# Splits ahead of the routing weights and norm roots by a GpSimd power in a two-layer mixture-of-experts encoder

## The chip, the cores and the metric

The kernel runs on one core of one Trainium2 chip. The metric is device time in microseconds (us) of a whole execution. TensorE (PE) multiplies matrices; VectorE (DVE), ScalarE (ACT) and GpSimd (POOL) work on tiles of 128 partitions; SyncE (SP) issues most of the transfers. Each engine takes its instructions in program order and waits where an input is missing.

## The reference, cut to what matters

512 tokens of width 1024 pass through two layers. In each, four attention mixers (`mla`, `dil`, `gqa`, `diff`) of four heads work on the normed input; their outputs are normed, joined, projected and added to the stream. A second norm feeds a router and 16 experts:

```
def rms_norm(x, gain):  x * rsqrt(mean(x * x) + 1e-6) * gain
...
g_prob = softmax(t @ wg + bg)                 # 4 groups: the best one is taken
e_logits = (t @ we + be)[best group]          # 4 experts in it: the best two
e_w, e_idx = top_k(softmax(e_logits), 2)
gate = one_hot(experts) * g_w * e_w / sum(e_w)
for e in range(16):
    hid = silu(t @ w_gate[e]) * (t @ w_up[e])
    y = y + gate[:, e:e + 1] * (hid @ w_down[e])
x = x + y
```

The weights are fp32: 1024 x 512 for gate and up, 512 x 1024 for down, per expert.

## The kernel before, in words

**Products.** Every fp32 product is three matmuls of a narrower type: each operand is split into a rounded `hi` and a rest `lo`, and `mm3` (L268) adds hi·hi, lo·hi and hi·lo. Weights arrive by SP's transfers in units of 128 x 1024 fp32 (`raw`). `W.split` turns the next units into `hi` (a copy on ACT, L144) and `lo` (a subtract, L145, on VectorE, or on POOL where it is called with G). It may run up to six units ahead of the unit in use (`HL`); a matrix of an expert is four units, and one unit is six matmuls.

**End of attention.** The order of the steps between the last attention units and the first expert is written by hand in `TAIL`: entries 57 to 69, run one after another by `tail`, each a list of words. A word is a letter, a token tile (0 to 3) and perhaps an engine (V or G): `o` and `d` open and close the out-projection of a tile, `r` is the root of the second norm, `e` the transposes for the router, `f` the router's logits, `h` the normed rows (`h30` a first part on POOL, `h31` the rest on ACT), `p` ranks the logits and counts each token's place in its expert's list, `x` picks the first expert's tokens by a matmul with a selection matrix, `l` makes the list of the second expert, `s` splits one unit, `T` splits the picked tokens into `xh` and `xl`, `K` computes the routing weights (`weights`, from L1333 to L1358), `m` clears a tile, `B` writes the last rows of the stream, `O` loads the number of overflow rounds into a register of each engine (L1470), `q` copies token numbers, `S` starts the gather of the second expert.

**Experts.** The matrices are worked through in the order g0 u0 g1 d0 u1 g2 d1 u2 and so on (`MOE_ORDER`; g is gate, u up, d down). Before each unit the loop splits ahead to the limit. At fixed units it makes the list of a later expert: `listed` forms the selection matrices (`hots`, four operations of L341), `start` multiplies them with the token numbers (`pli`, L1381), reads the list and gathers the rows. For every expert e this is done for e + 3 at u0 and u2. In expert 0 it is done beside that for expert 2 at g2 and u0, and for experts 0 and 1 (whose tokens have been picked already, but whose output rows and weights are still wanted) at u0 and u2.

**Roots.** `rstd` returns 1/sqrt(mean + eps) without ScalarE: a scale, an integer guess and three Newton rounds. The first three operations are on VectorE; the rounds are three operations each on VectorE (L133 to L135), or four each on POOL (L137 to L140) if E is G. It serves the first norm (`r0`, `r1`), the low-rank norm (`ra`), query and key heads (`rq`, 24 to 64 columns), the mixers' outputs (`yr`) and the second norm (`r2`). The third mixer's rope is on POOL (L430 to L445), behind VectorE's multiply by the root (L428). `kst` (L507) is a copy on POOL that TensorE transposes for the next head.

Of the kernel before, what the change touches and what calls it, by code (L numbers as in the profile page):

```python
# [44 lines left out]
        66: "e1 sG c2",  # L45
        67: "f0 b3G o2 p0 r1V f1 h1 d2 o3 r2G e2 x0 p1 c3 d3 f2 e3 h30 x1 r3G p2 h2 f3",
        68: "x2 h31 p3 l x3",
        69: "T K m sG B O q sG S"}
WAITP = 5
JOIN = 52  # L50
STORES = ((13, 0, 1), (6, 1, 2), (1, 2, 3), (0, 3, 4))
HOLD = 2
MIX = "gg" + "dg" * 8 + "gggggg"
CP = 704
# [8 lines left out]
def hybrid_encoder(ctx: ExitStack, tc: tile.TileContext, I: dict, out: bass.AP, depth=2, dbg=None):  # L63
# [18 lines left out]
    tokb = cst.tile([128, NT, 2], BF, name="tokb")  # L82
    wlast = cst.tile([128, NT], FT, name="wlast")
    brep = drm.tile([8, 128, 1024], FT, name="brep")

    def late_constants():
# [33 lines left out]

    def rstd(pool, ss, n, inv, name, E=V):

        x = "" if E is V else "g"
        v = pool.tile([128, n], FT, name=name + "v", tag="rsv" + x, bufs=1)
        y = pool.tile([128, n], FT, name=name + "y", tag=name + "y")
        f = pool.tile([128, n], FT, name=name + "f", tag="rsf" + x, bufs=1)
        ti = pool.tile([128, n], I32, name=name + "i", tag="rsi" + x, bufs=1)
        V.tensor_scalar(v, ss, inv, EPS, op0=OP.mult, op1=OP.add)
        V.tensor_scalar(ti, v.bitcast(I32), 1, None, op0=OP.logical_shift_right)
        V.tensor_scalar(y.bitcast(I32), ti, -1, 0x5f3759df, op0=OP.mult, op1=OP.add)  # L130
        for _ in range(3):
            if E is V:
                V.scalar_tensor_tensor(f, v, -0.5, y, op0=OP.mult, op1=OP.mult)  # L133
                V.tensor_tensor(f, f, y, op=OP.mult)
                V.scalar_tensor_tensor(y, f, 1.5, y, op0=OP.add, op1=OP.mult)  # L135
            else:
                E.tensor_tensor(f, y, y, op=OP.mult)  # L137
                E.tensor_tensor(f, f, v, op=OP.mult)
                E.tensor_scalar(f, f, -0.5, 1.5, op0=OP.mult, op1=OP.add)
                E.tensor_tensor(y, y, f, op=OP.mult)  # L140
        return y
# [181 lines left out]
    for layer in range(depth):  # L323
# [32 lines left out]
        with ExitStack() as c2:  # L356
# [425 lines left out]
            with ExitStack() as c3:  # L782
# [134 lines left out]
                def finish(mi):  # L917
# [3 lines left out]
                    if mi == 2:  # L921
# [3 lines left out]
                        yield LATER  # L925
                        r = rstd(sm, ss_, NT, 1.0 / 256, "yr", G)
                        for t in range(NT):
# [10 lines left out]
                    else:  # L938
                        for t in range(0, NT, 2):
# [3 lines left out]
                            V.tensor_reduce(ss_[:, t:t + 2], sq, axis=AX.X, op=OP.add)  # L943
                        r = rstd(sm, ss_, NT, 1.0 / 256, "yr", G)
                        yield LATER
# [12 lines left out]
                def finish_pair():  # L958

                    sl = slice(768, 896)  # L960
                    y = Y[3][:, :, :128]
                    yv = y.rearrange("p t (h d) -> p t h d", h=2)
                    sq = sm.tile([128, 512], FT, name="sq", bufs=1).rearrange("p (t h d) -> p t h d", t=NT, h=2)
                    ss_ = sm.tile([128, NT, 2], FT, name="yss")
                    G.tensor_tensor(sq, yv, yv, op=OP.mult)
                    yield LATER
                    V.tensor_reduce(ss_, sq, axis=AX.X, op=OP.add)
                    r = rstd(sm, ss_.rearrange("p t h -> p (t h)"), NT * 2, 1.0 / 64, "yr", G)
# [20 lines left out]
                def norm_pair(t, E):  # L989
                    sl, y = slice(896, 1024), Y[3][:, t, 128:]  # L990
                    r = rstd(sm, late['yss', t], 2, 1.0 / 64, "yr", E)
                    if E is V:
# [17 lines left out]
                def norm_x(t, E):  # L1010
                    V.tensor_scalar(ss2[:, t, 0:1], ss2[:, t, 0:1], ss2[:, t, 1:2], None, op0=OP.add)
                    late['r', t] = rstd(sm, ss2[:, t, 0:1], 1, 1.0 / D, "r2", E)

# [43 lines left out]
                def logits(t):  # L1057
                    pl = ps.tile([128, 512], FT, name="pl", tag="tr")[:, :20]
                    for k in range(8):
                        PE.matmul(pl, late['xT'][t % 2][:, k], late['wr'][:, k], start=k == 0, stop=k == 7)  # L1060
                    V.scalar_tensor_tensor(lg[:, t], pl, late['r', t], late['brg'][:, :20], op0=OP.mult, op1=OP.add)

# [25 lines left out]
                def route(t):  # L1088


                    l4 = lg[:, t].rearrange("p (r e) -> p r e", e=4)
# [5 lines left out]
                    for k, op in enumerate((OP.is_gt, OP.is_ge)):  # L1097
# [5 lines left out]
                    V.scalar_tensor_tensor(M[:, t].rearrange("p (g e) -> p g e", g=4), rank[:, t, 4:].rearrange("p (g e) -> p g e", g=4),  # L1103
                                           2.0, goh[:, t, :, None].to_broadcast([128, 4, 4]), op0=OP.is_lt, op1=OP.mult)
                    pp = ps.tile([128, 512], FT, name="pp", tag="tr")
                    for u in range(t + 1):
                        PE.matmul(pp[:, :NE], tri[:, 0 if u == t else 1], M[:, u], start=u == 0, stop=u == t)
# [5 lines left out]
                    V.tensor_scalar(late['oh'][:, t], iota, pos[:, t, 0:1], None, op0=OP.is_equal)  # L1113
                    if t == NT - 1:
                        oh1 = scr[:, 1536:1536 + NT * CAP // 2].bitcast(BF).rearrange("p (t c) -> p t c", t=NT)
                        late['oh1'] = hots(1, oh1)
                        count_rounds(pp[:, NE:2 * NE])

# [27 lines left out]

                STAGES = dict(l=list_rows, b=norm_pair, c=turn_pair, o=open_out, d=close_out, e=turn_x, r=norm_x, f=logits, h=normed,
                              p=route, x=pick, s=lambda E: W.split(W.done + 1, E), w=warm)
# [151 lines left out]
        with ExitStack() as c2:  # L1300
# [226 lines left out]
            for e, m in MOE_ORDER:  # L1527
                us = wbase[layer, e, m][0]
                for i, u in enumerate(us):
# [142 lines left out]
```

## Time and profile before

| | |
|---|---|
| median of three runs | 1393.4 us (1389.81 to 1403.58) |
| profiled execution | 1398.48 us |
| its span | 1396.6 us |
| mean granted TensorE clock | 0.966 of full speed |
| HBM read, written | 264.34 MB, 24.81 MB |

The rows below come from the profiled execution. Times are us from the start of its span; the span is the time between the first and the last instruction, and some 2 us of the execution lie around it. A timeline row gives start, busy time, engine, line of the kernel, operation, output and inputs, and in brackets the engine's idle time ahead of it with the instruction or queue that ended it. A name with q (ACTq) is an engine's sequencer: register loads and waits, not counted as busy. PEclk is the granted clock of TensorE, 1.00 for 2.4 GHz and 0.50 for 1.2 GHz.

### The profile page before, as it was taken

Reading aid. Unit: us, or ns where it says so; the run is one execution under the profiler, and the core shown is the slowest. Engines: PE = TensorE matmul, PEld = TensorE weight load, DVE = VectorE, ACT = ScalarE, POOL = GpSimd, SP = SyncE. Lnnn points to the kernel's source line nnn. Section 1 sums busy time; section 2 is a strip of 40 time slices with the busy share of each in tenths; the row PEclk is TensorE's granted clock in tenths of the full one; section 3 lists DMA queues with packets and bytes.
Section 4 is the critical chain, followed back from the end, with each engine's and each line's share of the span. In section 5 each row is a group of like instructions: output and inputs, shape, how many; then the busy total and the mean of one; then the engine's idle time right before and its main releaser. Section 6 shows DMA issues by size and latency. Waiting matters only on the chain.

```text
span 1396.6 us, 21240 instructions
## 1 busy us (share of the span) xinstructions
PE 1296.7 (93%) x7206; PEld 1024.0 (73%) x7206; DVE 1079.7 (77%) x2100; ACT 876.9 (63%) x1439; POOL 390.9 (28%) x670
## 2 busy tenths in 40 slices
PE   7999799999969999999989998999998799999996
PEld 6777688888846676666777877888886566676674
DVE  4648456879688999999876585678777799999994
ACT  3444346766347888888744444676744588888884
POOL 4205724313432111111032156332345121111120
PEclk8999879999989999999999998999999899999998
DMA  6344221011879999999444332110166899999960
GB/s 187 112 126 172 70 60 41 28 59 46 316 283 303 361 367 368 362 366 330 141 132 125 91 101 71 39 41 27 61 248 242 288 345 374 371 363 363 372 210 13
DMA packets 99935, 278.46 MB, mean 199 GB/s; under 512 B 18441, under 2 KB 29881, under 8 KB 99816
## 3 DMA queue, kind: packets, MB, share of 16 engines
q1 hardware_dynamic: 88888, 247.95, 49.8%
q0 software_dynamic: 10352, 27.41, 7.8%
q10 hardware_dynamic: 576, 1.64, 0.3%
q8 instruction: 59, 0.97, 0.3%
q14 instruction: 60, 0.49, 0.1%
HBM read 264.34 MB, written 24.81 MB: 207 GB/s over the span
## 4 chain that ended last, share of the span: by engine, by line
PE 25%; DMA 17%; DVE 14%; issue 9%; POOL 3%; ACT 3%; POOLq 0%; SPq 0%; ACTq 0%; DVEq 0%
PE pm L268 8%; DMA raw<-in_expert_w_up_dram 6%; DVE lo L145 6%; DMA raw<-in_expert_w_down_dram 5%; PE pd L268 5%; DMA raw<-in_expert_w_gate_dram 4%; PE pv L903 3%; PE ptr L276 3%; PE pu L268 2%; PE pg L268 2%; ACT hi L144 1%; DMA out_dram<-ye,ix 1%; ACT ye L1454 1%; DVE oh L341 1%; DMA x_sb<-in_expert_w_up_dram 1%
## 5 line engine op out<-in xcount | busy, mean ns | idle before, releaser
L145 DVE TENSOR_TENSOR lo<-raw,hi 128x1024 fp32r<-128x1024 f32 (+2 forms) x400 | 484.9, 1234 | 83.3 <-ACT hi L144 73.4
L144 ACT ACTIVATE hi<-raw 128x1024 fp32r<-128x1024 f32 (+1 forms) x410 | 422.5, 1050 | 93.1 <-PE pu L268 20.1
L268 PE MATMUL pm<-hi,hTh 128*128 128x512 f32 (+2 forms) x384 | 139.3, 363 | 9.5 <-DVE qkl L145 6.7
L268 PE MATMUL pm<-lo,hTh 128*128 128x512 f32 (+2 forms) x384 | 138.0, 359 | 5.4 <-DVE lo L145 5.4
L268 PE MATMUL pm<-hi,hTl 128*128 128x512 f32 (+2 forms) x384 | 138.2, 360 | 0.4
L268 PE MATMUL pg<-lo,xh 128*96 128x512 f32 x256 | 103.0, 402 | 7.1 <-POOL lo L145 4.6
L268 PE MATMUL pg<-hi,xh 128*96 128x512 f32 x256 | 104.4, 408 | 5.6 <-ACTq L1470 4.2
L268 PE MATMUL pu<-hi,xh 128*96 128x512 f32 (+1 forms) x272 | 108.9, 400 | 0.0
L268 PE MATMUL pd<-hi,hl 128*96 128x512 f32 x256 | 102.1, 399 | 4.5 <-DVE hl L145 4.5
L268 PE MATMUL pu<-lo,xh 128*96 128x512 f32 (+1 forms) x272 | 105.8, 389 | 0.0
L268 PE MATMUL pu<-hi,xl 128*96 128x512 f32 (+1 forms) x272 | 104.8, 385 | 0.0
L903 PE MATMUL pv<-v,pT 128*128 128x64 f32 x768 | 98.6, 271 | 6.5 <-DVE pT L891 2.7
L268 PE MATMUL pd<-lo,hh 128*96 128x512 f32 x256 | 101.2, 395 | 1.6 <-DVE lo L145 1.6
L903 PEld LDWEIGHTS pv<-v,pT 128*128 128x128 f32 x768 | 94.0, 193 | 10.6 <-DVE pT L891 4.7
L874 ACT ACTIVATE p<-p,m 128x512 f32<-128x512 f32 x96 | 68.7, 717 | 52.2 <-DVE m L856 51.9
L268 PE MATMUL pg<-hi,xl 128*96 128x512 f32 x256 | 101.5, 397 | 0.0
L268 PE MATMUL pd<-hi,hh 128*96 128x512 f32 x256 | 100.8, 394 | 0.0
L268 PEld LDWEIGHTS pm<-hi,hTh 128*128 128x128 f32 x384 | 75.0, 195 | 22.2 <-DVE qkl L145 7.6
L268 PEld LDWEIGHTS pm<-lo,hTh 128*128 128x128 f32 x384 | 75.0, 195 | 16.4 <-DVE lo L145 7.4
L276 PE MATMUL ptr<-ident,p 128*128 128x128 f32 x512 | 81.3, 283 | 5.8 <-ACT p L872 5.5
L276 PEld LDWEIGHTS ptr<-ident,p 128*128 128x128 f32 x512 | 67.0, 146 | 25.0 <-ACT p L872 6.4
L268 PEld LDWEIGHTS pm<-hi,hTl 128*128 128x128 f32 x384 | 75.1, 196 | 10.9 <-DVE hTl L145 2.1
(365 smaller groups left out, 2775.6 us busy)
## 6 DMA issues: line engine op xcount, KB each, us to landing
raw<-in_expert_w_down_dram SPq DMA_DIRECT2D x116, 512.0 KB
raw<-in_expert_w_gate_dram SPq DMA_DIRECT2D x114, 512.0 KB
raw<-in_expert_w_up_dram SPq DMA_DIRECT2D x112, 512.0 KB
raw<-in_w_in_dram SPq DMA_DIRECT2D x32, 512.0 KB
raw<-in_w_out_dram SPq DMA_DIRECT2D x16, 512.0 KB
toep<-brep SPq DMA_DIRECT2D x16, 448.0 KB
x_sb<-in_expert_w_gate_dram SPq DMA_DIRECT2D x14, 512.0 KB
x_sb<-in_expert_w_down_dram SPq DMA_DIRECT2D x12, 512.0 KB
```

The source lines that it names most:

```text
L144: A.activation(hi, src, AF.Copy)
L145: E.tensor_tensor(lo, src, hi.bitcast(FT), op=OP.subtract)
L268: PE.matmul(pt, a, b, start=first and n == 0, stop=last and n == tot - 1)
L276: PE.transpose(pt[:c, i * 128:(i + 1) * 128], s, ident)
L341: V.tensor_scalar(oh[:, t], iota, pos[:, t, e:e + 1], None, op0=OP.is_equal)
L874: A.activation(p, p, AF.Exp, bias=m, scale=-1.0, accum_out=s)
L903: PE.matmul(st['pv'][:, t], self.pT[:, k * 128:(k + 1) * 128], self.v(k), start=k == 0, stop=k == NT - 1)
L1454: A.activation(ye[:CAP, n * 512:(n + 1) * 512], self.pd[n], AF.Copy, scale=self.w)
```

## The change

- **Roots.** `rstd` is two operations on POOL for every use: a scale with the eps, and a power of −0.5 (against a constant tile `mhalf`). The argument E is gone.
- **Splits.** Unit 0 is split ahead of entry 66 in both. Before, units 1 and 2 followed on POOL, behind the routing weights (the two `sG` of entry 69), and units 3 and up on VectorE in the expert loop. Now units 1 to 5 are split on VectorE, in entries 67 (two), 68 (one) and 69 (two; a third call there finds the limit of six reached), all ahead of K.
- **Steps.** The logits' last operation (`g`, logged) and the places (`P`) are words of their own. The last tile's logits (f3) come ahead of the picks x1 to x3, h2 earlier, r3 ahead of h30. The second expert's selection matrices and the count of rounds (`N`), and its list (`l`), come after the last pick x3. The clearing `m` and the gather `S` come after the splits and ahead of K.
- **Lists.** Expert 2's selection matrices are formed at u0 unit 1 and its list at unit 3; expert 3's at g1 units 1 and 3; expert 4's at u1 units 0 and 2. Experts 0 and 1 get theirs at units 0 and 2 of their own down matrix.

```
-        67: "f0 b3G o2 p0 r1V f1 h1 d2 o3 r2G e2 x0 p1 c3 d3 f2 e3 h30 x1 r3G p2 h2 f3",
-        68: "x2 h31 p3 l x3",
-        69: "T K m sG B O q sG S"}
+        67: "f0 g0 b3G o2 p0 P0 r1V f1 g1 h1 d2 o3 r2G e2 sV x0 p1 P1 h2 c3 d3 r3G h30 f2 g2 e3 p2 f3 P2 g3 sV x1 p3 P3 x2 h31",
+        68: "x3 N l sV",
+        69: "T sV sV sV m S K B O q"}
+FIRST = ((2, ((0, 'u', 1), (0, 'u', 3))), (3, ((1, 'g', 1), (1, 'g', 3))), (4, ((1, 'u', 0), (1, 'u', 2))))
...
+    G.memset(mhalf, -0.5)
...
-    def rstd(pool, ss, n, inv, name, E=V):
+    def rstd(pool, ss, n, inv, name):
-        V.tensor_scalar(v, ss, inv, EPS, op0=OP.mult, op1=OP.add)
-        V.tensor_scalar(ti, v.bitcast(I32), 1, None, op0=OP.logical_shift_right)
-        V.tensor_scalar(y.bitcast(I32), ti, -1, 0x5f3759df, op0=OP.mult, op1=OP.add)
-        for _ in range(3):
-            if E is V:
-                V.scalar_tensor_tensor(f, v, -0.5, y, op0=OP.mult, op1=OP.mult)
-                V.tensor_tensor(f, f, y, op=OP.mult)
-                V.scalar_tensor_tensor(y, f, 1.5, y, op0=OP.add, op1=OP.mult)
-            else:
-                E.tensor_tensor(f, y, y, op=OP.mult)
-                E.tensor_tensor(f, f, v, op=OP.mult)
-                E.tensor_scalar(f, f, -0.5, 1.5, op0=OP.mult, op1=OP.add)
-                E.tensor_tensor(y, y, f, op=OP.mult)
+        G.tensor_scalar(v, ss, inv, EPS, op0=OP.mult, op1=OP.add)
+        G.tensor_tensor(y, v, mhalf.to_broadcast([128, n]), op=OP.pow)
...
+                def logged(t):
+                    V.scalar_tensor_tensor(lg[:, t], late['pl', t], late['r', t], late['brg'][:, :20], op0=OP.mult, op1=OP.add)
...
+                def next_list():
+                    oh1 = late['scr'][:, 1536:1536 + NT * CAP // 2].bitcast(BF).rearrange("p (t c) -> p t c", t=NT)
+                    late['oh1'] = hots(1, oh1)
+                    count_rounds(late['pp'][:, NE:2 * NE])
...
-                    for s, todo in ((e + 3, (('u', 0), ('u', 2))),) + (((2, (('g', 2), ('u', 0))),) if e == 0 else ()):
-                        if (m, i) in todo and s < NE:
-                            (start if (m, i) == todo[1] else listed)(s)
-                    if (e, m) == (0, 'u') and i in (0, 2):
-                        j = i // 2
-                        X[j].hots = hots(j, sm.tile([128, NT, CAP], BF, name="oh", bufs=2))
-                        X[j].lists(lambda t: parts[:, t, j], rows=j == 0)
+                    for s, todo in FIRST if e < 2 else ((e + 3, (('u', 0), ('u', 2))),):
+                        if e > 1:
+                            todo = [(e,) + w for w in todo]
+                        if (e, m, i) in todo and s < NE:
+                            (start if (e, m, i) == todo[1] else listed)(s)
+                    if m == 'd' and e < 2:
+                        if i == 0:
+                            X[e].hots = hots(e, sm.tile([128, NT, CAP], BF, name="oh", bufs=2))
+                        elif i == 2:
+                            X[e].lists(lambda t: parts[:, t, e], rows=e == 0)
```

## Rows read from the trace of the kernel before

**Rows 1.** The page: busy time, share of the span and instructions of each engine.

```profile
PE 1296.7 (93%) x7206; PEld 1024.0 (73%) x7206; DVE 1079.7 (77%) x2100; ACT 876.9 (63%) x1439; POOL 390.9 (28%) x670
```

**Rows 2.** Windows: busy us of PE, PEld, DVE, ACT, POOL (instructions), PEclk, DMA, GB/s.

```profile
226.60:230.00 3.40, 3.40 (x15) 3.10 (x15) 1.62 (x4) 0.89 (x2) 3.16 (x6) 0.50 0.00 0
340.00:389.00 49.00, 47.81 (x315) 41.44 (x315) 35.30 (x121) 19.54 (x52) 26.41 (x80) 1.00 0.64 248
394.00:427.00 33.00, 20.12 (x73) 12.81 (x74) 26.35 (x64) 16.71 (x20) 8.53 (x7) 0.81 0.89 327
427.00:440.00 13.00, 13.00 (x59) 9.11 (x58) 10.80 (x10) 10.55 (x13) 0.00 (x0) 0.96 0.85 260
450.00:650.00 200.00, 197.95 (x963) 138.66 (x962) 185.79 (x254) 165.94 (x198) 32.19 (x23) 1.00 1.02 364
1073.00:1106.00 33.00, 20.28 (x74) 12.93 (x74) 26.77 (x65) 17.02 (x21) 8.59 (x7) 0.81 0.90 328
```

**Rows 3.** Timeline of TensorE, first expert of layer 0 (start, busy, engine, instruction, idle).

```profile
394.59 0.45 PE L268 MATMUL pg<-hi,xh 128*96 128x512 f32 x1 [0.78 <-PEq L1470]
...
398.23 0.47 PE L268 MATMUL pg<-hi,xh 128*96 128x512 f32 x1 [2.02 <-ACTq L1470]
400.67 0.74 PE L268 MATMUL pg<-lo,xh 128*96 128x512 f32 x1 [1.97 <-POOL lo L145]
...
406.94 0.47 PE L268 MATMUL pg<-lo,xh 128*96 128x512 f32 x1 [1.39 <-DVE lo L145]
...
415.69 0.78 PE L1381 MATMUL pli<-parts,oh 128*96 128x5 bf16 x4 [3.27 <-DVE oh L341]
...
426.84 0.63 PE L268 MATMUL pg<-hi,xh 128*96 128x512 f32 x1
```

**Rows 4.** Timeline of VectorE in the same stretch.

```profile
387.92 0.24 DVE L1061 SCALAR_TENSOR_TENSOR lg<-pl,r2y,br 128x20 f32<-128x20 f32 x1 [0.64 <-POOL r2y L140]
...
394.38 0.56 DVE L145 TENSOR_TENSOR xl<-acc,xh 128x384 fp32r<-128x384 f32 x1 [0.28 <-ACT xh L144]
...
398.50 2.20 DVE L1328 TENSOR_TENSOR first<-gate,parts 128x64 f32<-128x64 f32 x1
400.74 3.17 DVE L1326 CAST parts<-first 128x64 bf16<-128x64 f32 x1
403.94 0.29 DVE L1328 TENSOR_TENSOR first<-first,parts 128x64 f32<-128x64 f32 x1
...
405.66 5.77 DVE L145 TENSOR_TENSOR lo<-raw,hi 128x1024 fp32r<-128x1024 f32 x5 [1.14 <-DVEq L1470]
411.35 0.81 DVE L341 TENSOR_SCALAR oh<-iota,pos 128x96 bf16<-128x96 f32 x4
...
424.60 1.22 DVE L145 TENSOR_TENSOR lo<-raw,hi 128x1024 fp32r<-128x1024 f32 x1
```

**Rows 5.** Timeline of GpSimd in the same stretch.

```profile
383.73 0.20 POOL L137 TENSOR_TENSOR r2f<-r2y 128x1 f32<-128x1 f32 x1 [0.50 <-DVE r2y L130]
...
387.69 0.19 POOL L140 TENSOR_TENSOR r2y<-r2y,r2f 128x1 f32<-128x1 f32 x1
...
398.26 2.35 POOL L145 TENSOR_TENSOR lo<-raw,hi 128x1024 fp32r<-128x1024 f32 x1 [7.22 <-ACTq L1470]
```

**Rows 6.** Timeline of GpSimd and TensorE around `kst` in layer 0.

```profile
225.94 0.61 POOL L507 COPY kst<-qk 128x512 f32<-128x512 f32 x1
...
226.60 1.11 PE L276 MATMUL ptr<-ident,kst 128*128 128x128 f32 x4 [1.62 <-POOL kst L507]
```

**Rows 7.** Timeline of VectorE and ScalarE around the third mixer's rope, layer 0.

```profile
133.86 0.18 DVE L128 TENSOR_SCALAR rqv<-ssq 128x24 f32<-128x24 f32 x1
...
137.47 3.40 DVE L428 TENSOR_TENSOR qk<-qk,rqy 128x256 f32<-128x256 f32 x8
...
165.94 0.69 ACT L872 ACTIVATE p<-sc,m 128x512 f32<-128x512 f32 x1 [8.52 <-POOL qk L444]
```

**Rows 8.** Timeline of VectorE in the fourth mixer's root, layer 0.

```profile
174.35 2.27 DVE L133 SCALAR_TENSOR_TENSOR rqf<-rqv,rqy 128x64 f32<-128x64 f32 x1
```

More of the change, by code (lines that the diff above doesn't have):

```diff
@@ L83, in hybrid_encoder @@
     wlast = cst.tile([128, NT], FT, name="wlast")
+    mhalf = cst.tile([128, 1], FT, name="mhalf")
     brep = drm.tile([8, 128, 1024], FT, name="brep")
+    G.memset(mhalf, -0.5)
     def late_constants():
@@ L118, in bias_steps @@
             SP.dma_start(brep, btd[:, None, :].to_broadcast([8, 128, 1024]))
-    def rstd(pool, ss, n, inv, name, E=V):
-        x = "" if E is V else "g"
-        v = pool.tile([128, n], FT, name=name + "v", tag="rsv" + x, bufs=1)
+    def rstd(pool, ss, n, inv, name):
+        v = pool.tile([128, n], FT, name=name + "v", tag="rsv", bufs=2)
         y = pool.tile([128, n], FT, name=name + "y", tag=name + "y")
-        f = pool.tile([128, n], FT, name=name + "f", tag="rsf" + x, bufs=1)
-        ti = pool.tile([128, n], I32, name=name + "i", tag="rsi" + x, bufs=1)
-        V.tensor_scalar(v, ss, inv, EPS, op0=OP.mult, op1=OP.add)
-        V.tensor_scalar(ti, v.bitcast(I32), 1, None, op0=OP.logical_shift_right)
-        V.tensor_scalar(y.bitcast(I32), ti, -1, 0x5f3759df, op0=OP.mult, op1=OP.add)
-        for _ in range(3):
-            if E is V:
-                V.scalar_tensor_tensor(f, v, -0.5, y, op0=OP.mult, op1=OP.mult)
-                V.tensor_tensor(f, f, y, op=OP.mult)
-                V.scalar_tensor_tensor(y, f, 1.5, y, op0=OP.add, op1=OP.mult)
-            else:
-                E.tensor_tensor(f, y, y, op=OP.mult)
-                E.tensor_tensor(f, f, v, op=OP.mult)
-                E.tensor_scalar(f, f, -0.5, 1.5, op0=OP.mult, op1=OP.add)
-                E.tensor_tensor(y, y, f, op=OP.mult)
+        G.tensor_scalar(v, ss, inv, EPS, op0=OP.mult, op1=OP.add)
+        G.tensor_tensor(y, v, mhalf.to_broadcast([128, n]), op=OP.pow)
         return y
@@ L925, in finish @@
                         yield LATER
-                        r = rstd(sm, ss_, NT, 1.0 / 256, "yr", G)
+                        r = rstd(sm, ss_, NT, 1.0 / 256, "yr")
                         for t in range(NT):
@@ L943, in finish @@
                             V.tensor_reduce(ss_[:, t:t + 2], sq, axis=AX.X, op=OP.add)
-                        r = rstd(sm, ss_, NT, 1.0 / 256, "yr", G)
+                        r = rstd(sm, ss_, NT, 1.0 / 256, "yr")
                         yield LATER
@@ L967, in finish_pair @@
                     V.tensor_reduce(ss_, sq, axis=AX.X, op=OP.add)
-                    r = rstd(sm, ss_.rearrange("p t h -> p (t h)"), NT * 2, 1.0 / 64, "yr", G)
+                    r = rstd(sm, ss_.rearrange("p t h -> p (t h)"), NT * 2, 1.0 / 64, "yr")
                     rv = r.rearrange("p (t h) -> p t h", t=NT)
@@ L990, in norm_pair @@
                     sl, y = slice(896, 1024), Y[3][:, t, 128:]
-                    r = rstd(sm, late['yss', t], 2, 1.0 / 64, "yr", E)
+                    r = rstd(sm, late['yss', t], 2, 1.0 / 64, "yr")
                     if E is V:
@@ L1011, in norm_x @@
                     V.tensor_scalar(ss2[:, t, 0:1], ss2[:, t, 0:1], ss2[:, t, 1:2], None, op0=OP.add)
-                    late['r', t] = rstd(sm, ss2[:, t, 0:1], 1, 1.0 / D, "r2", E)
+                    late['r', t] = rstd(sm, ss2[:, t, 0:1], 1, 1.0 / D, "r2")
                 def sq2():
@@ L1060, in logits @@
                         PE.matmul(pl, late['xT'][t % 2][:, k], late['wr'][:, k], start=k == 0, stop=k == 7)
-                    V.scalar_tensor_tensor(lg[:, t], pl, late['r', t], late['brg'][:, :20], op0=OP.mult, op1=OP.add)
+                    late['pl', t] = pl
+                def logged(t):
+                    V.scalar_tensor_tensor(lg[:, t], late['pl', t], late['r', t], late['brg'][:, :20], op0=OP.mult, op1=OP.add)
                 def normed(t, part=None):
@@ L1104, in route, with places @@
                                            2.0, goh[:, t, :, None].to_broadcast([128, 4, 4]), op0=OP.is_lt, op1=OP.mult)
+                def places(t):
+                    scr = late['scr']
                     pp = ps.tile([128, 512], FT, name="pp", tag="tr")
+                    late['pp'] = pp
                     for u in range(t + 1):
@@ L1113, in route @@
                     V.tensor_scalar(late['oh'][:, t], iota, pos[:, t, 0:1], None, op0=OP.is_equal)
[L1114 to L1117, printed above, removed]
+                def next_list():
+                    oh1 = late['scr'][:, 1536:1536 + NT * CAP // 2].bitcast(BF).rearrange("p (t c) -> p t c", t=NT)
+                    late['oh1'] = hots(1, oh1)
+                    count_rounds(late['pp'][:, NE:2 * NE])
                 def count_rounds(cnt):
@@ L1145, in list_rows @@
                     X[1] = bass.IndirectOffsetOnAxis(ap=ix[:CAP], axis=0)
-                STAGES = dict(l=list_rows, b=norm_pair, c=turn_pair, o=open_out, d=close_out, e=turn_x, r=norm_x, f=logits, h=normed,
+                STAGES = dict(l=list_rows, g=logged, P=places, N=next_list, b=norm_pair, c=turn_pair, o=open_out, d=close_out, e=turn_x, r=norm_x, f=logits, h=normed,
                               p=route, x=pick, s=lambda E: W.split(W.done + 1, E), w=warm)
```

## The prediction

> **What bounds the kernel now.** I read the page's busy times first. TensorE is busy 93% of the span, VectorE 77% [rows 1], so a change that only lightens VectorE can win only where TensorE waits for it. Busy time by window says where that is. From 450 to 650 us, in the run of the experts, TensorE works 197.95 of 200 us while VectorE has 185.79: TensorE bounds, with VectorE close behind (14 us to spare in 200, or 7%). From 340 to 389, at the end of attention, TensorE works 47.81 of 49. Between them, from 394 to 427, it works 20.12 of 33 at a mean clock of 0.81; right after, 13.00 of 13. The second layer repeats it: 20.28 of 33 [rows 2]. The stage to price is therefore the first expert of each layer, with some 13 us idle and more lost to the half clock.
>
> TensorE's timeline names each stall there [rows 3]. Unit 1 waits 2.02 us on ACT's queue, where its copy stands behind ACT's part of the routing weights; then 1.97 for a split that POOL makes, with a second one behind it; 1.39 for VectorE's first split; 3.27 for the selection matrices (`oh`) of the lists; gate 1 opens at 426.84. Two more list stalls of that pattern stand beside it (1.95 and 1.38). VectorE's timeline shows why [rows 4]: after the last `xl` (ends 394.94) it works through the routing weights until 404.52. Two of their small operations took 2.20 and 3.17 us where the twin of the first takes 0.29, and they end with POOL's two splits (the first runs 398.26 to 400.61 [rows 5]). So POOL's splits are slow themselves (2.35 us against 1.15 on VectorE) and hold VectorE some 4.8 us.
>
> **Part 1: splits ahead of the weights, lists spread.** I write VectorE's new order from the end of the last pick (393.81, that is 394.59 less its 0.78 idle [rows 3]). The list's matmuls cost 0.78 [rows 3]; split 3 one 1.15 (5.77 over 5); two `xl` 1.12; splits 4 and 5 2.30; the routing weights without blocking 9.6 − 4.8 = 4.8 (394.94 to 404.52, less 2.20 + 3.17, plus 2 × 0.29); the overflow's register load 1.14; splits 6 to 10 5.77; the second expert's two `xl` 1.12; one set of selection matrices 0.81; its matmuls 0.78 [rows 3, 4]. That is 19.8 us, so gate 1 opens at about 413.6 and with a few 0.1 us reads 414, against 426.84: **12.8 us** sooner. TensorE meanwhile has units 0 to 7 (eight of about 1.4 us, 11.2), list and overflow, and fits in the same time.
>
> It is not all kept. By 424.60 the old order had ten VectorE splits done (units 3 to 12, first and last in [rows 4]); mine has done through 10. Owed are two splits (2.3) and three sets of selection matrices (experts 3, 0 and 1, 2.4) that the lists' new places put behind gate 1: 4.7 us on an engine with 7% spare, or 1.3 us per expert of 18 [rows 2]. Some is hidden, because the split lead (six units) is cover; I count all of it, as the nearest pattern [rows 3] shows such sets straight in TensorE's way. A stall of some 4 us remains early, and after such stalls the trace has half clock stretches: one after the `kst` gap is 3.4 us long at 0.50 [rows 2], worth 1.7. So 12.8 − 4.7 − 1.7 = **6.4 us a layer**, with bounds of 0 (the lists stall again wherever they land) and 14.5 (debt hidden, clock regained).
>
> Logits of the last tile ahead of the picks: its `lg` waited 0.64 us for POOL's last root step [rows 4], and the root now comes some 3.5 us earlier. But POOL's two halves of h3 now follow the root, beside VectorE's routing operations with two inputs, and unit 2's split (1.15) stands in front of the last tile's routing. Bounds: 0.6 gained to 3 lost; the nearest rows are the blocked ones [rows 4]. I take 0.7 lost a layer. The memset and the first gather behind the splits on POOL cost nothing: with POOL's splits gone (4.7 us) POOL is idle there, and the gather feeds an expert that starts 20 us later; without that cover they would cost their own 2 us.
>
> **Part 2: roots by power.** The trace has no power operation. Its price lies between a POOL multiply (0.20 for one column) and the chain that it replaces (383.73 to 387.88, 4.1 us [rows 5]), or above if it works per column. I take 0.2 to 1.5, nearest to the multiply, since the first of the two new operations is one of that kind. Most roots are behind other work. Three are not:
> - The rope of the third mixer. ACT's first exponential waits 8.52 us for POOL's rope, which starts when VectorE's multiply at 137.47 has begun; that stands behind a root of 133.86 to 136.4 and one split (1.1) [rows 7]. With the root on POOL the split goes in its shadow: 1.5 us sooner in the first layer, 0.2 in the second, whose split has no input earlier. Together 1.7.
> - `kst`, a POOL copy, starts at 225.94 behind the twelve root steps and TensorE waits 1.62 for it [rows 6], then runs 3.4 us at 0.50 [rows 2]. The pattern has two gaps, one each layer, the second without half clock: 2 × 1.62 + 1.7 = 4.9. It vanishes if a four-column power is under 2 us, and comes back past that.
> - The fourth mixer's 64-column root on VectorE, held 2.27 us by a POOL split [rows 8]. On POOL it queues behind that split: between 4 lost and 4 gained; I take 0.
>
> The first root of three columns stands ahead of thirteen DMA issues on POOL, which go some 5 us later. The splits of the in-projection's units, which stand ahead of the tables' first readers on VectorE, hide that; if this cover went, it would cost up to 5 us in each layer.
>
> A 128 x 1024 subtract takes 2.35 us on POOL [rows 5] and 1.15 on VectorE [rows 4], 2.0 times; the rows thus speak for part 1 and against part 2, unless fewer steps outweigh it, and here two stand for twelve. The Trainium skill, GPSIMD Engine Reference, section 4.1, sends elementwise work to VectorE, since POOL is about 2 times slower with two inputs. The trace agrees for the subtract; no run here shows a power. Were a power worth twice VectorE's whole root (2.56 us [rows 7], so an estimate of 5.1 by that page), the sum would go by rival 3, to 10 × (5.1 − 3.3) − 11.4 = 6.6 above, 1400.
>
> **Sum.** 2 × (6.4 − 0.7) + 1.7 + 4.9 = 18.0 us, or 1.3%. Against the profiled execution (1398.48, of which 1396.6 is span and 1.9 lies around it) that is about 1380.5; this execution stands 5 above the median of the three runs, 1393.4, so the median after would be **1375**.
>
> **The rivals.**
> 1. *The stall only moves.* VectorE owes the same work in the first two experts; the lists of experts 2, 3 and 0 stop TensorE later instead of now. For it: 185.79 of 200 busy [rows 2] gives no room to repay. Against: POOL's blocking of 4.8 us is real work removed. Only 0 to 1 a layer and the roots' 6.6 would stay: about 1386.
> 2. *The whole head start is kept.* The debt of 4.7 is hidden under a TensorE that bounds, and the clock stays up: 2 × (14.5 − 0.7) + 6.6 + up to 4 from the 64-column root = 34 to 38, about 1358. For it: 13.00 of 13 busy after gate 1 with the splits only a few units ahead [rows 2]. Against: the old order had a lead of four units there, the new one two.
> 3. *Slow power, slower than before.* If power runs per column at some hundred ns, each root on the path (first norm, third and fourth mixers, `kst`, last tile: five a layer, ten in all) costs its price above the 3.3 us mean of the chains removed (2.56 on VectorE [rows 7], 4.15 on POOL [rows 5]). Without the 6.6 of part 2 the rest gains 11.4, so it decides from 3.3 + 1.1 = 4.4 us a root; at 6 us it gives 27 − 11.4 = 16 above, 1409. For it: no row shows a power; against: POOL's steps of one to four columns are all 0.2 to 0.6.
> 4. *The change doesn't do what it says*: the split ahead is limited to six units, and two of them use buffers that the norm's gain and the turned tiles held before; if these come free late, two splits go behind the weights again, 2.3 a layer, about 1380.
>
> **How the numbers follow.** Forecast of 1375 (1366 to 1382, and rival 4 within it) 0.46; rival 1 (1382 to 1396) 0.25; rival 2 (1350 to 1366) 0.20; rival 3 (1397 up) 0.09. The range leaves out most of rival 3 and the lower half of rival 2: 1357 to 1396. A measurement of this kernel can tell about 1% from no change, so faster means under 1379.5: 0.20 and most of 0.46, 0.60 in all; slower (over 1407) 0.07; the rest, 0.33, within.
>
> **What the changed profile would show.** POOL's splits gone before gate 1, and the routing weights on VectorE done in about 5 us with no operation over 0.5. No TensorE wait for a POOL split; the first `oh` wait nearer 411 than 415.69; gate 1 near 414, and from there more idle than the 13.00 of 13. The 1.62 for `kst` gone in both layers; the rope's multiply 1.5 sooner. A power row in all of it, under 1.5 us. Wrong it would be if TensorE idles more than 5 us between gate 1 and the fourth expert's gate (rival 1), if it idles none (rival 2), or if a power row is over 2 us (rival 3).

## The result and the profile after

The changed kernel takes 1441.4 us (median of 4 runs, 1440.5 to 1442.6) against 1391.9 for the kernel before: 1.032 times as long, 95% interval 1.029 to 1.035. The forecast was 1375. The profiled execution's span is 1439.3 us against 1396.6, 42.7 longer.

The page, span and busy times (compare [rows 1]): VectorE has 54 us less to do, POOL 39 more, TensorE 7 more, and the span grows all the same.

```profile
span 1439.3 us, 20791 instructions
...
PE 1303.5 (91%) x7206; PEld 1031.9 (72%) x7206; DVE 1025.3 (71%) x1828; ACT 875.6 (61%) x1439; POOL 429.8 (30%) x503
```

Where the 42.7 went can be read from the starts of the same matmuls in both traces, in three stretches of each layer:

| stretch | layer 0 | layer 1 |
|---|---|---|
| start of the layer to the first router logits | +12.0 | +16.8 |
| first logits to the first matmul of expert 0 | +7.2 | +7.5 |
| from there to the layer's last down matmul | −0.3 | −0.3 |

The last line is a sum of two: 3.2 and 2.8 us won by gate 1, 2.9 and 2.5 lost behind it.

The first line can only be the roots, since the order ahead of the logits is the old one (pow_all, below, tests it). The grouped instructions of line 129, the power, each width apart (count, then busy us and mean ns of one):

```profile
L129 POOL TENSOR_TENSOR rqy<-rqv,mhalf 128x32 f32<-128x32 f32 x4 | 21.7, 5424 | 0.3
...
L129 POOL TENSOR_TENSOR rqy<-rqv,mhalf 128x64 f32<-128x64 f32 x2 | 21.1, 10527 | 0.2
...
L129 POOL TENSOR_TENSOR rqy<-rqv,mhalf 128x24 f32<-128x24 f32 x2 | 8.3, 4154 | 0.2
...
L129 POOL TENSOR_TENSOR yry<-yrv,mhalf 128x4 f32<-128x4 f32 x6 | 6.1, 1011 | 0.5
...
L129 POOL TENSOR_TENSOR yry<-yrv,mhalf 128x2 f32<-128x2 f32 x8 | 5.8, 731 | 0.7
...
L129 POOL TENSOR_TENSOR r2y<-r2v,mhalf 128x1 f32<-128x1 f32 x8 | 4.5, 564 | 0.7
```

A power takes 0.56 us for one column and 0.16 more for each further one: 4.2 us for 24 columns, 5.4 for 32, 10.5 for 64. The twelve operations of [rows 7] took 2.6 for 24. The VectorE and TensorE timelines show who waits in layer 0 (in brackets the idle time and what ended it):

```profile
148.76 3.39 DVE L417 TENSOR_TENSOR qk<-qk,rqy 128x256 f32<-128x256 f32 x8 [2.38 <-POOL rqy L129]
...
198.70 0.76 DVE L417 TENSOR_TENSOR qk<-qk,rqy 128x256 f32<-128x256 f32 x2 [12.96 <-POOL rqy L129]
...
201.31 1.97 PE L892 MATMUL pv<-vm,pT 128*128 128x64 f32 x8 [11.04 <-DVE pT L880]
```

The multiply by the third mixer's root starts at 148.76 instead of 137.47 [rows 7], 11.3 us later. Of these 4.9 are there from the first 70 us on (pow_narrow, below, shows why), 5.5 come from the two 32-column roots ahead of it, and 0.9 from its own root. The fourth mixer's root, 64 columns wide, holds VectorE for 12.96 us and TensorE for 11.04. The 1.62 us for `kst` [rows 6] are gone in both layers.

The second line is the new order of steps. The windows of after, columns as in [rows 2]: from the first logits to expert 0, then expert 0 to gate 1, what follows, the steady run, and expert 0 of layer 1.

```profile
374.90:413.80 38.90, 35.28 (x214) 31.64 (x213) 20.60 (x63) 11.02 (x24) 10.86 (x18) 0.82 0.51 198
413.80:442.80 29.00, 14.53 (x60) 9.56 (x61) 16.36 (x43) 13.73 (x18) 2.31 (x3) 0.82 0.81 295
442.80:456.00 13.20, 13.20 (x62) 9.19 (x62) 12.98 (x25) 8.61 (x10) 4.65 (x2) 0.88 0.93 298
470.00:670.00 200.00, 197.76 (x967) 138.75 (x968) 185.81 (x257) 164.20 (x196) 33.48 (x23) 1.00 1.01 363
1116.80:1146.00 29.20, 13.14 (x61) 8.75 (x61) 16.41 (x43) 13.88 (x18) 2.77 (x3) 0.82 0.80 295
```

TensorE has about the work that it had there before, but its clock is 0.82 in the first of these rows, where the trace of before granted 1.00 until the end of the picks. The steady run is what it was (197.76 busy of 200, [rows 2]). Expert 0 still has half of its time idle: 14.53 busy of 29. TensorE's timeline, to be read beside [rows 3]:

```profile
392.43 0.17 PE L1103 MATMUL pp<-M,tri 128*128 128x16 bf16 x1 [2.60 <-DVE M L1094]
...
413.77 0.45 PE L257 MATMUL pg<-hi,xh 128*96 128x512 f32 x1
...
415.68 0.47 PE L257 MATMUL pg<-hi,xl 128*96 128x512 f32 x1 [1.23 <-DVE xl L134]
...
424.23 0.45 PE L257 MATMUL pu<-hi,xh 128*96 128x512 f32 x1 [3.24 <-DVEq L1468]
...
442.21 0.78 PE L1379 MATMUL pli<-parts,oh 128*96 128x5 bf16 x4 [10.00 <-DVE oh L330]
442.84 0.72 PE L257 MATMUL pg<-hi,xh 128*96 128x512 f32 x1
```

POOL's splits are gone from the brackets, and the gate matmuls of expert 0 follow each other but for 1.23 us. Two new waits stand in their place: 3.24 us for VectorE to pass the overflow branch (line 1468), and 10.00 at the list. The list is only the next in line; VectorE itself had been idle, as its timeline and ScalarE's show:

```profile
389.73 1.23 DVE L134 TENSOR_TENSOR lo<-raw,hi 128x1024 fp32r<-128x1024 f32 x1 [3.54 <-ACT hi L133]
...
418.37 0.15 DVE L1331 TENSOR_REDUCE mxg<-lg 128x4 f32<-128x16 f32 x1
...
424.24 3.50 DVE L134 TENSOR_TENSOR lo<-raw,hi 128x1024 fp32r<-128x1024 f32 x3 [1.14 <-DVEq L1468]
438.68 2.36 DVE L134 TENSOR_TENSOR lo<-raw,hi 128x1024 fp32r<-128x1024 f32 x2 [10.95 <-ACT hi L133]
...
435.82 1.28 ACT L1417 ACT_TABLE_LOAD   x1 [10.30 <-SPq L1468]
```

Unit 1's split, now ahead of a ranking, waits 3.54 us for its ScalarE copy (389.73); the ranking's matmul pays 2.60 for it (392.43 above). The routing weights take 5.9 us with the register load (418.37 to 424.24), as forecast, with no blocked operation. Then VectorE waits 10.95 us for ScalarE's copies, which stand behind the silu of expert 0, and the silu waits 10.30 us for SyncE to leave the overflow branch. SyncE's timeline and the DMA engines' (40 slices of 0.65 us from 414 to 440; busy tenths, then GB/s):

```profile
415.18 1.75 SPq L172 DMA_DIRECT2D raw<-in_expert_w_down_dram  x4
417.02 2.20 SPq L175 DMA_DIRECT2D raw<-in_expert_w_up_dram  x4
419.33 0.57 SPq L175 DMA_DIRECT2D raw<-in_expert_w_gate_dram  x1
421.45 0.33 SPq L175 DMA_DIRECT2D x_sb<-in_expert_w_gate_dram  x1
424.40 11.78 SPq L175 DMA_DIRECT2D raw<-in_expert_w_gate_dram  x2
```

```profile
DMA  0009699998899999999999999999975200079899
GB/s 0 0 0 132 183 365 403 403 246 177 271 334 384 429 410 416 429 410 416 435 410 403 416 410 410 429 410 410 403 296 214 76 25 0 0 126 296 340 410 416
```

The early splits free weight buffers, and SyncE issues eleven transfers of 512 KB in 415 to 424.7, ahead of the branch in its queue; the twelfth, which the last row groups with the eleventh, follows at 435.8. In between, the DMA engines run full until about 433 and are empty from about 435. The silu's table load starts at 435.82. What SyncE does at the branch stands in the rows of that line (counts, durations in ns, first and last start, over both layers):

```profile
L1468 SPq EVENT_SEMAPHORE  x16: 17/17/17, 430.8 to 1138.8; - x16
...
L1468 SPq COMPARE_BRANCH  x2: 50/52/53, 425.7 to 1128.8; - x2
```

Behind the compare at 425.7 it passes eight semaphore waits in each layer. The trace has their times and those of the landings: in layer 0 the first passes at 430.8, though its transfer had landed at 426.3, and the last four, from 431.9 to 435.7, each pass within 0.02 us of a landing. So the ten us have two halves: about five in which SyncE waits for no transfer (what it does there no row shows; in the kernel before it is 5.9), and five for the transfers.

### The profile page after: what moved, and what is told of

It reads as the page before. It is cut to its first block, busy times and chain, and to the rows that moved or that the text cites. A ratio compares the mean times of both kernels' runs of the same rounds, so it can differ in the third digit from the quotient of the medians.

```text
span 1439.3 us, 20791 instructions
## 1 busy us (share of the span) xinstructions
PE 1303.5 (91%) x7206; PEld 1031.9 (72%) x7206; DVE 1025.3 (71%) x1828; ACT 875.6 (61%) x1439; POOL 429.8 (30%) x503
## 5 line engine op out<-in xcount | busy, mean ns | idle before, releaser
L134 DVE TENSOR_TENSOR lo<-raw,hi 128x1024 fp32r<-128x1024 f32 (+1 forms) x404 | 489.6, 1233 | 110.6 <-ACT hi L133 103.6
```

The lines of the kernel that those rows point to most:

```text
L134: E.tensor_tensor(lo, src, hi.bitcast(FT), op=OP.subtract)
```

## The experiments

Each was compared with runs of the kernel before on the same chip (medians of 1394.5 to 1396.4 there). One execution of the same code can be 9 us ahead of another by the end of attention, so steps within a stretch are compared, not starts.

**pow_all**: the kernel before with the new `rstd`, order and lists as they were.

```
-        V.tensor_scalar(v, ss, inv, EPS, op0=OP.mult, op1=OP.add)
...
+        G.tensor_scalar(v, ss, inv, EPS, op0=OP.mult, op1=OP.add)
+        G.tensor_tensor(y, v, mhalf.to_broadcast([128, n]), op=OP.pow)
```

> Roots theory: a power costs about 0.24 us plus 0.16 us a column (0.56 us for 1 column, 5.42 for 32, 10.5 for 64 in the profile after), so that the four wide query and key roots of each layer stand in TensorE's way. The first logits came 12.0 us later in the first layer and 16.8 us more in the second, and nothing else of the change lies ahead of them: with the old order kept, 1392 + 29 = 1421 us. Rival, that the powers are mostly hidden and the new order carries the loss: within 7 us of 1392.

Measured: 1426.8 us, ratio 1.021 (1.018 to 1.024), 30 us above. The powers alone cost what the first stretches said.

**order_only**: the changed kernel with the Newton rounds.

```
-        G.tensor_tensor(y, v, mhalf.to_broadcast([128, n]), op=OP.pow)
...
+        for _ in range(3):
+            if E is V:
+                V.scalar_tensor_tensor(f, v, -0.5, y, op0=OP.mult, op1=OP.mult)
...
```

> The new order and lists with the Newton roots of before. Theory that both parts lose by themselves: from the first logits to the first matmul of expert 0 the profile after lost 7.2 and 7.5 us, and from there to the third expert it won under 1 us a layer: 1392 + 14 = 1406 us. Rival, that all of the loss is the power and the order alone wins what was forecast: 1381 us.

Measured: 1407.9 us, ratio 1.007 (1.005 to 1.010), 11.5 above. Both parts lose by themselves, and nearly add: 30 + 11.5 = 41.5, where the ratio of 1.032 for both together makes 45. From the first logits to expert 0 this run's trace loses 8.9 and 8.1 us. The silu waits as in the changed kernel (ScalarE's timeline):

```profile
423.49 1.28 ACT L1431 ACT_TABLE_LOAD   x1 [10.18 <-SPq L1482]
```

**pow_narrow**: the old order, a power for up to 8 columns, Newton rounds for the query and key roots.

```
+        if n <= 8:
+            G.tensor_scalar(v, ss, inv, EPS, op0=OP.mult, op1=OP.add)
+            G.tensor_tensor(y, v, mhalf.to_broadcast([128, n]), op=OP.pow)
+            return y
```

> The old order; a power for roots of up to 8 columns, Newton rounds for the wider ones. By the roots theory a narrow power (0.56 to 1.66 us) is cheaper than the chains of 2.5 to 4.1 us that it replaces, the 1.62 us wait for the kst copy goes in both layers, and the time is 1385 to 1390 us. Rival, that a power on GpSimd costs at any width: 1395 us or more.

Measured: 1393.6, ratio 0.998 (0.996 to 1.000), between the two theories; so the 30 us of pow_all lie in the wide roots. After 70 us the trace is 4.8 us late, and it makes up 7.8 from there to its end. GpSimd's timeline and ScalarE's for the start:

```profile
29.36 0.86 POOL L128 TENSOR_TENSOR r1y<-r1p,mhalf 128x3 f32<-128x3 f32 x1
30.18 0.81 POOL L392 DMA_DIRECT2D mla_q_norm_g<-in_mla_q_norm_g_dram  x1
...
45.46 1.06 ACT L152 ACTIVATE hi<-raw 128x1024 fp32r<-128x1024 f32 x1 [7.89 <-DMA raw<-in_w_in_dram]
```

POOL's table transfers begin at 30.18, behind the first norm's power, instead of 25.8; a weight transfer issued at 36.5 meets them, and ScalarE waits 7.89 us for it, against 2.56 before.

**pow_late**: the same, but only for the mixers' output roots and the second norm's.

```
-        if n <= 8:
+        if name in ('yr', 'r2'):
```

> The old order, a power for the roots of the mixers' outputs and the second norm alone. pow_narrow lost 4.8 us in the first 70 us of the first layer, where the first norm's power on GpSimd holds back thirteen table transfers until they meet the weights (the weight transfer issued at 36.5 took 9 us to land), and won 7.6 us after that. Theory: the 4.8 come back: 6 to 9 us below the kernel before. Rival, that the start is only a draw of that execution: no more than 3 below.

Measured: 1387.9, ratio 0.993 (0.990 to 0.995), 7.6 below: the start's loss is gone (0.7 ahead after 70 us, and the same copy waits 2.42).

**order_defer**: order_only with the loads set free by the early splits held until after the branch (`z` stops loading, `y` takes it up).

```
-        69: "T sV sV sV m S K B O q"}
+        69: "z T sV sV sV m S K B O y q"}
```

> As order_only, but the weight transfers that the five early splits set free are issued after the overflow branch instead of ahead of it. Theory: SyncE leaves the branch only when the transfers issued ahead of it have landed, ScalarE's silu waits for that (10.3 us), and so do the weight copies behind it; then the wait shrinks to under 2 us, gate 1 comes some 10 us sooner in each layer, and the time is 1406 - 20 = 1386 us. Rival, that VectorE's backlog of splits and lists is what holds gate 1: the silu goes sooner, gate 1 moves by under 2 us, and the time stays at 1403 to 1406.

Measured: 1405.4, ratio 1.005 (1.002 to 1.008), 9 above the kernel before. Only three of the eleven transfers moved behind the branch; the other eight belong to the loading that is taken up at the end of attention, and stayed. ScalarE's and TensorE's rows:

```profile
420.24 1.28 ACT L1431 ACT_TABLE_LOAD   x1 [6.68 <-SPq L1482]
...
426.63 0.78 PE L1393 MATMUL pli<-parts,oh 128*96 128x5 bf16 x4 [7.90 <-DVE oh L344]
```

Counted from the first gate matmul, the silu starts 3.5 us sooner than in order_only, and gate 1 as much (3.3 in the second layer; the idle time ahead of the list goes from 11.4 to 7.9). The direction agrees with the theory. Its size was far too large, since eight transfers and SyncE's five us without one stayed, and the rival isn't excluded by it.

**order_own**: order_only with the branch's load tile and its PSUM buffers apart from the experts'.

```
-                    r = sm.tile([128, 512], FT, name="sg", bufs=1)
-                    SP.dma_start(r, w)
+                    for n in range(2):
+                        r = sm.tile([128, 256], FT, name="ow", bufs=1)
+                        SP.dma_start(r, w[:, n * 256:(n + 1) * 256])
...
-                            x.pu = pq.tile([128, FF], FT, name="pu", tag="pv")[:CAP]
+                            x.pu = pq.tile([128, FF], FT, name="pu", tag="sc")[:CAP]
...
```

> order_only, but the overflow branch has a load tile of its own (half as wide, two loads) and the PSUM buffers of the down products, so that neither the silu nor the first up matmul has to wait until SyncE and VectorE have passed the branch. The transfers keep their order. Theory: ScalarE's 10 us wait ahead of the silu, the 3.2 us wait of the up matmul and most of the 11.4 us gap ahead of gate 1 go, and gate 1 comes 10 to 13 us sooner in each layer: 9 to 14 us below the kernel before. Rival, that VectorE's splits and lists hold gate 1 anyway, as the run with deferred transfers (gate 1 only 3.3 us sooner) may also be read: gate 1 moves by under 4 us a layer, still 4 to 11 above.

Measured: 1405.5, ratio 1.007 (1.004 to 1.009), 10 above. The miss has a visible cause:

```profile
410.01 0.71 PE L271 MATMUL pg<-hi,xh 128*96 128x512 f32 x1 [10.59 <-DVEq L1483]
...
417.88 1.28 ACT L1431 ACT_TABLE_LOAD   x1
```

The silu no longer waits, but the other PSUM buffers make the very first gate matmul wait 10.59 us for VectorE to pass the branch. The line of `gu` that names an expert's buffers, the same in all versions, shows why:

```
pool, tag = (pq, "pv") if m == 'u' else (ps, "mm") if self is not X[0] else (pq, "sc")
```

Expert 0's gate product takes a buffer of `sc`, where this edit put the branch's products; up products take one of `pv`, which the branch uses in every version without this edit. Here the up matmul, which waits 3.21 us in order_only, doesn't wait. **before_own**, the same edit in the kernel before, shows that wait too (12.0 us there):

> The kernel before with the overflow branch's own tile and PSUM buffers. Its silu waits only 2.5 us for SyncE, and its gate 1 comes 16 us after that behind VectorE: 0 to 3 us below the kernel before. If the branch were costly in any order: 8 or more below.

Measured: 1400.3, ratio 1.005 (1.002 to 1.008), slower, which neither reading expected; it tests the PSUM edit and not the tile.

**order_tile**: order_only with the tile alone.

```
-                    r = sm.tile([128, 512], FT, name="sg", bufs=1)
-                    SP.dma_start(r, w)
+                    for n in range(2):
+                        r = sm.tile([128, 256], FT, name="ow", bufs=1)
+                        SP.dma_start(r, w[:, n * 256:(n + 1) * 256])
...
```

> order_only with only the load tile of the overflow branch changed (its own, half as wide); the PSUM buffers stay. The run with other PSUM buffers had the silu free of its wait, but the first gate matmul then waited 10.6 us for VectorE to pass the branch, and gate 1 still came 5.7 us sooner than in order_only. Theory: now neither wait is there except the up matmul's 3.2 us; the gap ahead of gate 1 falls from 11.4 us to under 2, gate 1 comes 9 to 11 us sooner in each layer, and with the clock kept the time is 7 to 12 us below the kernel before (order_only: 11.5 above). Rival, that VectorE's lists and splits hold it next: a gap of 4 us or more at the lists remains and the time is 0 to 6 above.

Measured: 1393.1, ratio 0.998 (0.997 to 1.000), 2.4 below the kernel before, between theory and rival, and 15 below order_only by the medians, 12 by the ratios. TensorE and ScalarE:

```profile
409.07 0.45 PE L271 MATMUL pu<-hi,xh 128*96 128x512 f32 x1 [1.65 <-DVEq L1483]
...
415.67 0.48 PE L271 MATMUL pu<-lo,xh 128*96 128x512 f32 x1 [1.31 <-DVE lo L148]
...
420.18 0.78 PE L1393 MATMUL pli<-parts,oh 128*96 128x5 bf16 x4 [3.11 <-DVE oh L344]
420.82 0.72 PE L271 MATMUL pg<-hi,xh 128*96 128x512 f32 x1
...
410.37 1.28 ACT L1431 ACT_TABLE_LOAD   x1
```

The table load of the silu starts with no wait, and from the first gate matmul to gate 1 it is 22.2 us instead of 29.0 in order_only (18.5 against 29.7 in layer 1). In layer 0 waits of 3.11 at the list and 1.31 for a split remain, as the rival had it; in layer 1 only 1.39 at the list. Both had a share.

**before_tile**: the kernel before with that tile.

> The kernel before with only the load tile of the overflow branch its own. If SyncE's wait in the branch mattered only because the new order put ten transfers ahead of it, the silu is 2.5 us sooner and nothing waits for that: within 3 us of the kernel before. If the branch held the old order as well: 5 or more below.

Measured: 1394.7, ratio 1.001 (0.999 to 1.004): nothing. The silu of the old order waited 2.47 us for SyncE in the kernel before and doesn't here, but in layer 0 nothing had waited for the silu: gate 1 comes 32.2 us after the first gate matmul with and without the tile. (In layer 1 of this trace it comes 2.5 us sooner; the times don't show it.) The silu's row:

```profile
397.42 1.28 ACT L1419 ACT_TABLE_LOAD   x1
```

**order_move**: order_only with two splits behind the steps that they had stood ahead of.

```
-"... r2G e2 sV x0 p1 P1 h2 c3 d3 r3G ... P2 g3 sV x1 p3 P3 x2 h31"
+"... r2G e2 x0 p1 P1 h2 c3 sV d3 r3G ... P2 g3 x1 p3 P3 x2 sV h31"
```

> order_only (11.5 us above the kernel before) with two splits moved: unit 1 from ahead of the second pick to behind the last pair's transpose, unit 2 from ahead of the last tile's ranking to behind it. Theory: unit 1's split stood ahead of a ranking, waited 3.5 us for ScalarE, and TensorE lost 2.60 us plus 17 us at half clock; 7.0 us in the first layer and 7.7 in the second go: 3 us below the kernel before. Rival, that the logits ahead of the picks cost this by themselves: still 10 to 12 above.

Measured: 1403.9, ratio 1.007 (1.004 to 1.009), 4 below order_only by the medians and still 8.6 above the kernel before, so between theory and rival. In the trace the stretch from the first logits to expert 0 gives back 4.2 and 3.4 of the 8.9 and 8.1 us, about half. The other half stays and is told below.

**both_late**: order_move and order_own together, with the power for the late roots.

> The new order with both mends (moved splits, own tile), and a power only for the roots of the mixers' outputs and of the second norm (1 to 8 columns). Theory: the parts add, -14 for the moved splits, -20 to -26 for the branch, -6 to -8 for the roots from +11.5: 30 us below the kernel before, 22 to 37. Rival, that VectorE's debt of the first two experts, which stood behind the branch's stall unseen, now stops TensorE: 5 to 15 below.

Measured: 1385.2, ratio 0.994 (0.992 to 0.995), 10 below; the PSUM wait of 10.59 is in it.

**both_tile**: order_tile, the moved splits and the late powers.

> order_tile with the two splits moved and the power only for the mixers' output roots and the second norm's. Theory: below both_late (-10) by the wait of the first gate matmul, 10.6 less 3.2 in each layer, and some of its half clock: 25 to 30 us below the kernel before. Rival, that the wait only moves to the up matmul and the lists: 10 to 15 below.

Measured: 1373.9, ratio 0.984 (0.982 to 0.986), 21.6 below, between theory and rival. It is the fastest here and beats both kernels. The late powers alone brought 7.6 (pow_late), so the order with its mends brings some 14. Its TensorE, and its windows:

```profile
384.76 0.44 PE L277 MATMUL pg<-hi,xh 128*96 128x512 f32 x1
...
395.22 0.45 PE L277 MATMUL pu<-hi,xh 128*96 128x512 f32 x1 [1.67 <-DVEq L1489]
...
402.91 0.74 PE L1399 MATMUL pli<-parts,oh 128*96 128x5 bf16 x4 [1.27 <-DVE oh L350]
403.51 0.45 PE L277 MATMUL pg<-hi,xh 128*96 128x512 f32 x1
```

```profile
349.00:384.80 35.80, 33.72 (x216) 30.47 (x214) 21.19 (x64) 11.12 (x24) 11.06 (x18) 0.86 0.56 220
384.80:403.50 18.70, 14.53 (x60) 9.45 (x61) 16.35 (x43) 13.72 (x18) 2.29 (x3) 0.91 0.87 326
```

From the first gate matmul (384.76) to gate 1 it takes 18.7 us, where the kernel before took 32.25 [rows 3].

**tile_oldlists**: both_tile with the lists of before.

```
-                    for s, todo in FIRST if e < 2 else ((e + 3, (('u', 0), ('u', 2))),):
+                    for s, todo in ((e + 3, (('u', 0), ('u', 2))),) + (((2, (('g', 2), ('u', 0))),) if e == 0 else ()):
...
```

> both_tile (21.6 us below the kernel before) with the lists of the first two experts put back where they were: experts 2, 0, 3 and 1 all at the last gate unit and the up units of expert 0. Theory: the spread is a part of the gain of its own, since VectorE now has as many splits and two or three more sets of selection matrices ahead of gate 1; the lists stop TensorE for 4 to 7 us at up units 0 to 2, gate 1 comes that much later, and 1 to 3 us of it come back after gate 1: 14 to 18 below the kernel before. Rival, that the early splits alone give the lead: within 2 us of both_tile.

Measured: 1384.3, ratio 0.993 (0.991 to 0.996), 10.3 below, so 11 slower than both_tile (13 by the ratios). The three list stalls are back:

```profile
399.37 0.74 PE L1399 MATMUL pli<-parts,oh 128*96 128x5 bf16 x4 [1.00 <-DVE oh L350]
403.42 0.78 PE L1399 MATMUL pli<-parts,oh 128*96 128x5 bf16 x4 [3.31 <-DVE oh L350]
...
411.48 0.74 PE L1399 MATMUL pli<-parts,oh 128*96 128x3 bf16 x4 [1.21 <-DVE oh L350]
```

## Why the prediction was wrong

**The power's price.** The step that failed: "I take 0.2 to 1.5, nearest to the multiply". For the narrow widths that nearly holds (0.56 to 1.66 us), for the wide ones it was off by three to seven times, since the price goes by the column. The text had that as rival 3, with 0.09, and the evidence against it there ("POOL's steps of one to four columns are all 0.2 to 0.6") spoke for narrow steps alone. (Two steps of 240 on POOL, both of two columns, took 1.05.) The rival's own sum was wrong in form as well: ten equal roots, where four wide ones a layer carry the loss. pow_all shows the effect apart, 30 us. Its sign, "a power row ... over 2 us", is there: 4.15 to 10.53.

The wide roots reverse two of the three terms of part 2. The rope came 11 us later, not 1.5 sooner; 5.5 of them are the two 32-column roots ahead of it, which "Most roots are behind other work" put at nothing. The 64-column root, taken as 0 between 4 lost and 4 gained, left TensorE idle for 11.04 us and put its matmuls 8.7 further behind in layer 0. `kst` was right: its wait is gone, and in pow_narrow and in pow_late the stretch with it is 3.5 us shorter in the first layer and 2.1 in the second, 5.6 where 4.9 were forecast.

The Trainium skill, GPSIMD Engine Reference, section 4.1, sends elementwise work on a tile to VectorE (its row names add, multiply and max, not a power), and by that the root would belong there. The trace agrees for the wide roots (4.15 us for the power of 24 columns, 2.56 for the twelve VectorE operations [rows 7]) and not for one or two columns (0.56 and 0.73), where two operations beat twelve.

**The table transfers.** "The splits of the in-projection's units ... hide that; if this cover went, it would cost up to 5 us in each layer." It went in the first layer only: the changed kernel is 5.0 us late after its first 70 us (pow_narrow 4.8), and 1.0 over the same part of the second. What it cost was not the tables' readers, as assumed, but a weight transfer that they held up.

**The end of attention.** Forecast 0.7 lost, measured 7.2 and 7.5. "Unit 2's split (1.15) stands in front of the last tile's routing" was priced, unit 1's place ahead of the second tile's routing was not, nor that a split on VectorE waits for a ScalarE copy: 2.60 us of TensorE. Moving both splits gave back half of what order_only loses there (4.2 and 3.4 of 8.9 and 8.1). The rest goes with the clock: both_tile still loses 3.9 and 3.6 us, and in its first layer 10.2 us at half clock remain (0.86 in its first window), which cost 5.1, with idle times of only 0.80 and 0.96 in TensorE's way. They lie in a stretch where logits and picks now follow each other; the old order had them among the projection's matmuls. No run tried that order apart, so this cause is only argued.

**The first expert.** The ledger gave 12.8 us to gate 1; the changed kernel won 3.2 and 2.8. The step that failed: "TensorE meanwhile has units 0 to 7 ..., list and overflow, and fits in the same time". It counted VectorE and TensorE, but not the transfers that each moved split issues on SyncE ahead of the branch, nor ScalarE, whose silu shares a tile with the branch. With that tile apart and the splits moved, the ledger's number comes out: 13.5 us in the first layer and 12.0 in the second (both_tile). The transfers' part is shown by SyncE's waits at the landings, the silu's by order_tile. POOL's blocking of 4.8 went as forecast.

**The debt.** Counted 4.7 and 1.7 for the clock; in both_tile TensorE gives back 2.7 and 3.9 after gate 1. So the debt lay between the forecast and rival 2, and far from rival 1, but only once the branch was out of the way. From the first logits to the last down matmul both_tile's trace gains 11.4 us, both layers together and with the late powers in it, as much as the forecast's 2 × (6.4 − 0.7). That is luck: the debt was counted some 3 us a layer too high, and the end of attention some 3 too low. The spread lists are worth 11 us by tile_oldlists, more than the 4 to 7 expected: with the old lists the three waits of 1.00, 3.31 and 1.21 come back with half clock behind two of them.

**Open.** What SyncE does in the five us between its compare and the first semaphore wait, and why the clock falls at the end of attention. The waits of the first gate and up matmuls for VectorE are explained by their buffers (order_own): the up matmul's 1.3 to 3.2 us come with `pv`, and the order of before doesn't have them, as VectorE is past the branch there before the up product begins.

## What to carry to other kernels

Price an operation that the trace doesn't show by its widest use, or measure one of that width; a bound from narrow rows says nothing of it. A step that is moved takes its transfers along, so look through every queue for what they now stand ahead of, above all a branch. A buffer that a branch names, even one never entered, ties its next user to the passage of the engines that use it there; a small tile of the branch's own was worth 12 to 15 us once the order made that passage late, and nothing before.

## What the runs showed of the hardware

- A GpSimd power has a price per column: 0.56 us at 1, 1.01 at 4, 4.15 at 24, 5.42 at 32, 10.53 at 64, so about 0.4 + 0.16 for each.
- SyncE left the skipped branch at 435.7 us, ten us after its compare. It passed eight semaphore waits there: the first 5.1 us after the compare, the last four each at the landing of a transfer issued ahead of the branch. With three fewer ahead of it (order_defer) the silu behind it started 3.5 us sooner, counted from the first gate matmul.
- ScalarE waited 7.89 us for a 512 KB weight transfer issued while POOL's thirteen table transfers were under way, 2.4 to 2.6 without.
- At the end of attention TensorE ran at half clock for 10.2 us (both_tile) with waits of only 0.80 and 0.96 there, where the order of before kept 1.00 through waits of 0.56 and 1.18.
